# RG-LRU gate products: the two 64-feature blocks on the two halves of TensorE's rows

## Chip, cores and metric
The kernel runs on one core of one Trainium2 chip. The metric is device microseconds of one execution. In the profile PE is TensorE (PEld its weight loads), DVE is VectorE, ACT is ScalarE, POOL is GpSimd, and SP issues nearly all DMAs.

## Reference
A two-layer trunk over 256 latent and 256 context tokens with 2048 features. Each layer normalizes and modulates, projects into three branches, and projects back with a gated residual. The change touches the first branch, the RG-LRU, whose 512 features stand in 8 blocks of 64:

```python
ub = u.reshape(bsz, t_len, N_BLK_A, BLK_A)
gate_r = sigmoid(einsum('btni,nij->btnj', ub, w_r).reshape(bsz, t_len, D_A) + b_r)
gate_i = sigmoid(einsum('btni,nij->btnj', ub, w_i).reshape(bsz, t_len, D_A) + b_i)
log_a = -LRU_C * gate_r * softplus(-lam)
a = exp(log_a)
b = sqrt(-expm1(2.0 * log_a)) * (gate_i * u)
...
h = associative_scan(a * h + b)
```

Each gate multiplies every block of 64 features of u by a 64x64 matrix of its own. This is done for two directions of time and two layers. u is the branch's input after a convolution over four tokens.

## The kernel before
All tensors lie with features on the 128 partitions and the 512 tokens (256 latent, 256 context) on the free axis. A branch of 512 features is four tiles t, and a tile holds two of the 64-feature blocks.

*Projections.* `project` makes one tile of 128 output features from 16 input tiles. The weights come in chunks of 512 columns, four to a tile (`Weights.ahead`, three chunks ahead). ACT casts a chunk to a high half `wh`, DVE makes the low half `wl`, and each of four input tiles takes three matmuls (`accumulate`): wh by xh, wl by xh, wh by xl, all in the kernel's reduced fp32 type (F32R). In layer 1 the tiles that need no context stream 256 tokens in place of 512 (narrow tiles).

*Background work.* Between pairs of input tiles, `between` lets `Background.pump` run one step of each of three lanes: gated DeltaNet heads (lane 0), attention heads and RG-LRU tiles (lane 1), the short preparations (lane 2). The steps are Python generators, and each `yield` ends one. Which step runs where is decided by a cost model of the engines' clocks (class `Timed`). It also lets DVE fill its spare time with the products of the modulation weights (`macc`). The tile framework then orders the instructions of each engine by its own estimates. All instructions are recorded in one helper, so the profile puts them on line 89 and they are told apart by tile names.

*RG-LRU.* `consume` calls `rglru` (line 945) when one of the tiles xa0 to xa3 is projected. It runs the convolution on ACT and DVE, loads the gate weights `rgt`, and queues `rglru_scan` (line 951) in lane 1. That splits u into two halves `us` and, for each direction d, the weights into two halves `rg`. For each gate g, `product3` makes three matmuls of 128 rows, 128 columns and 512 tokens into a PSUM bank `pg` (pool `pb`, two banks), and ACT reads the bank with a tanh and the bias `hb`:

```python
for g, dst in ((0, a), (1, gu)):
    pg = pb_()
    product3(pg, [x[:, P * g:P * g + P] for x in rg], us)
    act.activation(out=dst, in_=pg, func=AF.Tanh, scale=0.5, bias=hb[:, 8 * g + j:8 * g + j + 1])
    yield
```

The weights of a gate are a 128x128 matrix with the two blocks on its diagonal and zeros elsewhere (`w_rg` in `kernel`). After the gates come a tanh (`m2sp`) and an exp (`m4sp`) on ACT, products on DVE, one Sqrt on ACT for both directions (with a table load before it), and the scans over time on DVE. There are 16 such groups of two gates: 2 layers, 4 tiles, 2 directions.

Of the kernel before, what the change touches and what calls it, by code (L numbers as in the profile page):

```python
# [10 lines left out]
AF = mybir.ActivationFunctionType  # L11
ALU = mybir.AluOpType

P = 128
KT = 16
T = 256
TT = 512
# [77 lines left out]
def trunk(ctx, tc, xT, cT, consts, masks, rope_t, small, fg, w_mod0, w_mod, w_first, w_in, w_ba, w_rg, w_out, out):  # L95
    nc = tc.nc
    pe, dve, act, pool = Timed(nc.tensor, "pe"), Timed(nc.vector, "dve"), Timed(nc.scalar, "act"), Timed(nc.gpsimd, "pool")
# [9 lines left out]
    def psum(tag, shape=(P, TT), bufs=2):  # L107
        return ps.tile(list(shape), F32, tag=tag, name=tag, bufs=bufs)
# [3 lines left out]
    def tmp(tag, shape=(P, TT), bufs=None, dt=F32):  # L112
        return wk.tile(list(shape), dt, tag=tag, name=tag, bufs=bufs or BUFS.get(tag, 2))
# [7 lines left out]
    def pb_():  # L121
        return psum("pb", bufs=2)
# [18 lines left out]
    for k in range(KT):  # L141
        y = big.tile([P, TT], F32, tag=f"Y{k}", name=f"Y{k}")
# [217 lines left out]
    def split(a, hi=None, lo=None):  # L360

        n = a.shape[1]
        hi = tmp("wb", dt=F32R)[:, 0:n] if hi is None else hi
        lo = tmp("wb", dt=F32R)[:, 0:n] if lo is None else lo
        act.copy(out=hi, in_=a)
        dve.tensor_tensor(out=lo, in0=a, in1=hi.bitcast(F32), op=ALU.subtract)
        return hi, lo

    def product3(out, a, b):

        for i, (x, y) in enumerate(((0, 0), (1, 0), (0, 1))):
            pe.matmul(out=out, lhsT=a[x], rhs=b[y], start=(i == 0), stop=(i == 2))
# [60 lines left out]
    def conv(pz, wc, halves, bias=None, tag="u"):  # L433
        n = len(halves)
        act.copy(out=zp[:, 0:n, 2:2 + T], in_=pz[:, 0:n * T].rearrange("p (s t) -> p s t", s=n))
        u = tmp(tag)
        uv = u[:, 0:n * T].rearrange("p (s t) -> p s t", s=n)
        if bias is None:
            act.activation(out=uv, in_=zp[:, 0:n, 0:T], func=AF.Copy, scale=wc[:, 0:1])
        else:  # L440
            act.activation(out=uv, in_=zp[:, 0:n, 0:T], func=AF.Identity, scale=wc[:, 0:1], bias=bias)
        for j in range(1, 4):
            dve.scalar_tensor_tensor(out=uv, in0=zp[:, 0:n, j:j + T], scalar=wc[:, j:j + 1], in1=uv, op0=ALU.mult, op1=ALU.add)
        return u
# [158 lines left out]
    def layer(l, acc, bs):  # L603
# [22 lines left out]
        hb = big.tile([P, 16], F32, tag="hb", name="hb")  # L626
# [11 lines left out]
        def yt(k):  # L638
            if ydst[k] is None:
                Y[k] = big.tile([P, TT], F32, tag=f"Y{k}", name=f"Y{k}")  # L640
                ydst[k] = Y[k]
            return ydst[k]
# [4 lines left out]
        def branch_result(k, src, cc, scale=None):  # L647

            ready.add(k)
            y = yt(k)[:, cc]  # L650
            if k in gated:
                dve.scalar_tensor_tensor(out=y, in0=src, scalar=0.5 if scale is None else scale, in1=y, op0=ALU.mult, op1=ALU.mult)
            elif scale is None:
                act.copy(out=y, in_=src)
            else:
                act.activation(out=y, in_=src, func=AF.Copy, scale=scale)
# [287 lines left out]

        def rglru(t, pz):
            u = conv(pz, s[:, S_CA + 4 * t:S_CA + 4 * t + 4], (0, 1), bias=s[:, S_CAB + t:S_CAB + t + 1], tag="wb")
            rgt = tmp("wa")
            nc.sync.dma_start(out=rgt, in_=w_rg[l, t].rearrange("p d g j -> p (d g j)"))
            bg.add(1, t, rglru_scan(t, u, rgt))

        def rglru_scan(t, u, rgt):
            us = split(u)
            th = tmp("th", (P, 2, TT), bufs=1)
            ab = []
            for d in range(2):
                j = 4 * d + t
                rg = tmp("wb", dt=F32R)
                rg = split(rgt[:, T * d:T * d + T], rg[:, 0:T], rg[:, T:TT])
                yield
                a, gu = tmp("wb"), tmp("wb")  # L960
                for g, dst in ((0, a), (1, gu)):
                    pg = pb_()
                    product3(pg, [x[:, P * g:P * g + P] for x in rg], us)
                    act.activation(out=dst, in_=pg, func=AF.Tanh, scale=0.5, bias=hb[:, 8 * g + j:8 * g + j + 1])
                    yield
                dve.scalar_tensor_tensor(out=gu, in0=gu, scalar=1.0, in1=u, op0=ALU.add, op1=ALU.mult)
                act.activation(out=th[:, d], in_=a, func=AF.Tanh, scale=m2sp[:, j:j + 1], bias=m2sp[:, j:j + 1])
                act.activation(out=a, in_=a, func=AF.Exp, scale=m4sp[:, j:j + 1], bias=m4sp[:, j:j + 1])
                dve.scalar_tensor_tensor(out=a, in0=a, scalar=1.0, in1=th[:, d], op0=ALU.add, op1=ALU.mult)
                dve.tensor_scalar(out=a, in0=a, scalar1=1.0, scalar2=None, op0=ALU.add)  # L970
                ab.append((a, gu))
                yield
            act.activation(out=th, in_=th, func=AF.Sqrt, scale=-1.0, bias=tiny)
            yield
            for d, (a, b) in enumerate(ab):
                dve.scalar_tensor_tensor(out=th[:, d], in0=a, scalar=1.0, in1=th[:, d], op0=ALU.add, op1=ALU.mult)
                dve.scalar_tensor_tensor(out=b, in0=b, scalar=0.5, in1=th[:, d], op0=ALU.mult, op1=ALU.mult)
                yield
                hh = th[:, d]
                if d == 0:  # L980
                    dve.tensor_tensor_scan(out=hh[:, T:TT], data0=a[:, T:TT], data1=b[:, T:TT], initial=0.0, op0=ALU.mult, op1=ALU.add)
                    dve.tensor_tensor_scan(out=hh[:, 0:T], data0=a[:, 0:T], data1=b[:, 0:T], initial=hh[:, TT - 1:TT], op0=ALU.mult, op1=ALU.add)
                else:
                    for a0, ini in ((T, 0.0), (0, hh[:, T:T + 1])):
                        r = lambda x: x[:, a0:a0 + T][:, ::-1]
                        dve.tensor_tensor_scan(out=r(hh), data0=r(a), data1=r(b), initial=ini, op0=ALU.mult, op1=ALU.add)
                yield
            if t in gated:
                dve.tensor_tensor(out=th[:, 0, 0:nq], in0=th[:, 0, 0:nq], in1=th[:, 1, 0:nq], op=ALU.add)
                branch_result(t, th[:, 0, 0:nq], slice(0, nq))  # L990
            else:
                dve.tensor_tensor(out=yt(t), in0=th[:, 0, 0:nq], in1=th[:, 1, 0:nq], op=ALU.add)
                ready.add(t)
# [166 lines left out]
        for n in range(KT):  # L1160
# [5 lines left out]
            if last:  # L1166
                y = Y[n][:, 0:T]
# [14 lines left out]
    for k in range(KT):  # L1182
        square_into(acc, Y[k], k, TT, dve)
    gw = []
    acc = layer(0, acc, None)
    mod_finish(((1, 0), (1, 1)))
    acc = layer(1, acc, gw[0])
# [86 lines left out]
```

## Time and profile before

| | us |
|---|---|
| median of 3 runs (1531.92 to 1535.7) | 1533.33 |
| the profiled execution | 1529.33 |
| its span on the core | 1527.5 |
| PE busy | 1466.9 |
| DVE busy | 1165.8 |
| ACT busy | 739.9 |
| mean granted TensorE clock | 0.994 |

The span goes from the first to the last instruction, and 1.8 us of the execution lie outside it. A timeline row gives the start of a group of equal instructions and how long they took from the first start to the last end. Matmuls overlap their neighbours, so the distance between two starts tells what one costs in a stream, not its duration. The RG-LRU tiles run from about 590 to 700 us (layer 0) and from 1340 to 1420 us (layer 1).

### The profile page before, as it was taken

The numbers are of one execution on the slowest core, as the hardware profiler recorded it, in microseconds if no ns is written. First come the engines' busy times: TensorE is split into PE (matmuls) and PEld (weight loads), VectorE is DVE, ScalarE is ACT, GpSimd is POOL, SyncE is SP. The second block draws the span as 40 slices with busy tenths as digits, with TensorE's granted clock in tenths as the row PEclk, the third lists the DMA queues.
The fourth block names the chain that finished last, engine by engine and source line by source line (L and its number), as shares of the span: only waits on it lengthen the run. The fifth ranks groups of instructions, "written<-read, shape, count | busy, mean of one in ns | idle before, by whom it ended". The sixth has DMA issues, their size and how long they took to land.

```text
span 1527.5 us, 29952 instructions
## 1 busy us (share of the span) xinstructions
PE 1466.9 (96%) x11762; PEld 1206.4 (79%) x11762; DVE 1165.8 (76%) x2513; ACT 739.9 (48%) x1708; POOL 113.2 (7%) x114
## 2 busy tenths in 40 slices
PE   4999999999999999999999999999999999999996
PEld 3777678787877877788888887877977889779996
DVE  4445989889898898999648876887885776788755
ACT  3323445454444546655422224554544555677653
POOL 0000100100010010000011110010200100000011
PEclk9999999999999999999999999999999999999998
DMA  9997544444443453345446655545552333234553
GB/s 345 332 347 256 152 127 144 128 135 130 144 149 113 145 177 116 107 143 160 136 127 224 212 188 196 187 146 170 183 178 64 104 115 104 81 98 131 190 189 113
DMA packets 90686, 247.68 MB, mean 162 GB/s; under 512 B 9200, under 2 KB 20912, under 8 KB 90544
## 3 DMA queue, kind: packets, MB, share of 16 engines
q1 hardware_dynamic: 89392, 244.71, 49.2%
q8 instruction: 92, 1.51, 0.4%
q10 hardware_dynamic: 1152, 1.05, 0.2%
q14 instruction: 50, 0.41, 0.1%
HBM read 243.60 MB, written 2.13 MB: 161 GB/s over the span
## 4 chain that ended last, share of the span: by engine, by line
PE 82%; DVE 10%; ACT 3%; DMA 2%; issue 1%; POOL 1%; SPq 0%; DVEq 0%; ACTq 0%; POOLq 0%
PE pz L89 58%; PE pa L89 9%; PE pb L89 8%; PE pt L89 4%; PE pm L89 3%; DVE wb L89 2%; DVE wl L89 1%; DVE macc L89 1%; DMA wraw<-in_w_in 1%; DVE th L89 1%; DVE o L89 1%; ACT t L89 1%; ACT wb L89 1%; DMA wa<-rows_d 1%; DVE u L89 1%
## 5 line engine op out<-in xcount | busy, mean ns | idle before, releaser
L89 PE MATMUL pz<-xh,wh 128*128 128x512 f32 (+1 forms) x1760 | 645.1, 367 | 2.5 <-ACT xh L89 2.4
L89 PE MATMUL pz<-xh,wl 128*128 128x512 f32 (+1 forms) x1760 | 629.4, 358 | 0.8 <-DVE wl L89 0.8
L89 PE MATMUL pz<-xl,wh 128*128 128x512 f32 (+1 forms) x1760 | 628.8, 357 | 0.0
L89 ACT CAST wh<-wraw 128x512 fp32r<-128x512 f32 x488 | 293.1, 612 | 335.5 <-PE pz L89 206.2
L89 DVE TENSOR_TENSOR wl<-wraw,wh 128x512 fp32r<-128x512 f32 x488 | 328.2, 681 | 133.0 <-ACT wh L89 131.7
L89 PEld LDWEIGHTS pz<-xh,wh 128*128 128x128 f32 x1760 | 331.8, 189 | 53.0 <-ACT xh L89 8.6
L89 PEld LDWEIGHTS pz<-xl,wh 128*128 128x128 f32 x1760 | 331.9, 189 | 50.4 <-DVE xl L89 3.5
L89 PEld LDWEIGHTS pz<-xh,wl 128*128 128x128 f32 x1760 | 332.6, 189 | 42.5 <-DVE wl L89 1.2
L89 DVE SCALAR_TENSOR_TENSOR macc<-wm,cs,macc 128x512 f32<-128x512 f32 x400 | 293.3, 766 | 2.1 <-DMA wm<-in_w_mod 1.6
L89 PE MATMUL pb<-wb 128*128 128x128 f32 (+1 forms) x560 | 112.5, 328 | 3.8 <-ACT wb L89 2.0
L89 PEld LDWEIGHTS pb<-wb 128*128 128x128 f32 x560 | 79.6, 190 | 16.9 <-ACT wb L89 7.0
L89 DVE TENSOR_SCALAR modA<-pm,nb,small 128x2 f32<-128x2 f32 x16 | 4.5, 279 | 69.2 <-PE pm L89 69.2
L89 POOL TENSOR_TENSOR o<-o,t 128x512 f32<-128x512 f32 (+1 forms) x28 | 30.4, 1086 | 325.7 <-ACT t L89 325.7
L89 ACT ACTIVATE wb<-pb,mx,rqa 128x512 f32<-128x512 f32 (+1 forms) x48 | 33.9, 707 | 42.4 <-DVE mx L89 42.1
L89 DVE SCALAR_TENSOR_TENSOR u<-zp,small,u 128x512 f32<-128x512 f32 (+1 forms) x72 | 50.6, 702 | 1.9 <-ACT u L89 1.6
L89 ACT ACTIVATE xh<-u,modS 128x256 fp32r<-128x256 f32 x64 | 30.9, 506 | 39.7 <-DVE u L89 39.6
L89 ACT ACTIVATE t<-pt 128x128 f32<-128x128 f32 (+1 forms) x122 | 34.2, 280 | 32.8 <-PE pt L89 30.7
L89 PEld LDWEIGHTS pa<-c,s 32*32 32x32 f32 x2304 | 24.9, 107 | 21.8 <-issue 13.0
L89 ACT COPY s<-pm 128x128 f32<-128x128 f32 x16 | 4.3, 266 | 67.0 <-PE pm L89 67.0
L89 DVE TENSOR_REDUCE mx<-pb 128x1 f32<-128x512 f32 (+1 forms) x48 | 28.8, 599 | 10.0 <-PE pb L89 9.6
L89 POOL TENSOR_TENSOR rqa<-rqa,mhalf 128x4 f32<-128x4 f32 (+1 forms) x16 | 17.3, 1084 | 243.6 <-DVE rqa L89 243.6
L89 ACT COPY wb<-pb 128x512 f32<-128x512 f32 (+1 forms) x48 | 24.7, 515 | 21.4 <-PE pb L89 20.9
(260 smaller groups left out, 1816.8 us busy)
## 6 DMA issues: line engine op xcount, KB each, us to landing
wraw<-in_w_in SPq DMA_DIRECT2D x148, 512.0 KB, 3.6
wm<-in_w_mod SPq DMA_DIRECT2D x128, 512.0 KB, 3.7
wraw<-in_w_out SPq DMA_DIRECT2D x64, 512.0 KB, 3.6
wraw<-in_w_first SPq DMA_DIRECT2D x32, 448.0 KB, 5.0
wb<-in_w_mod SPq DMA_DIRECT2D x48, 256.0 KB, 6.3
kq<-in_w_mod SPq DMA_DIRECT2D x16, 512.0 KB, 6.3
Y<-in_xT SPq DMA_DIRECT2D x16, 256.0 KB, 5.4
wa<-in_w_mod SPq DMA_DIRECT2D x16, 256.0 KB, 6.8
```

The source lines that it names most:

```text
L89: return f(*args, **kw)
```

## The change
A gate no longer fills a 128x128 matrix with two blocks and zeros. For each block b (the rows 64b to 64b + 63) the weights are now 64 rows by 128 columns, one gate's 64 columns beside the other's: gate r first for block 0, gate i first for block 1. Three matmuls on the upper half of TensorE's rows go into one PSUM bank, and three on the lower half (`tile_position` 64) into the other. The two halves take turns. A bank then holds both gates of one block, so ACT reads each gate in two halves of 64 partitions. For gate i each half is read from the other half's partitions, and the biases are rolled to match. The number of matmuls stays at 96, the tanh reads go from 32 to 64, and the gate weights halve, which also halves their loads (8 DMAs), their casts (16) and their low halves (16). The yields stay as many; the first step now holds all six matmuls.

```diff
@@ -944,9 +944,11 @@
 
         def rglru(t, pz):
             u = conv(pz, s[:, S_CA + 4 * t:S_CA + 4 * t + 4], (0, 1), bias=s[:, S_CAB + t:S_CAB + t + 1], tag="wb")
-            rgt = tmp("wa")
-            nc.sync.dma_start(out=rgt, in_=w_rg[l, t].rearrange("p d g j -> p (d g j)"))
+            rgt = tmp("wa")[:, 0:2 * P]
+            nc.sync.dma_start(out=rgt, in_=w_rg[l, t].rearrange("p d j -> p (d j)"))
             bg.add(1, t, rglru_scan(t, u, rgt))
+
+        halves = (slice(0, 64), slice(64, P))
 
         def rglru_scan(t, u, rgt):
             us = split(u)
@@ -955,14 +957,22 @@
             for d in range(2):
                 j = 4 * d + t
                 rg = tmp("wb", dt=F32R)
-                rg = split(rgt[:, T * d:T * d + T], rg[:, 0:T], rg[:, T:TT])
+                rg = split(rgt[:, P * d:P * d + P], rg[:, 0:P], rg[:, P:2 * P])
                 yield
                 a, gu = tmp("wb"), tmp("wb")
-                for g, dst in ((0, a), (1, gu)):
-                    pg = pb_()
-                    product3(pg, [x[:, P * g:P * g + P] for x in rg], us)
-                    act.activation(out=dst, in_=pg, func=AF.Tanh, scale=0.5, bias=hb[:, 8 * g + j:8 * g + j + 1])
-                    yield
+
+
+                pg = [pb_(), pb_()]
+                for i, (x, y) in enumerate(((0, 0), (1, 0), (0, 1))):
+                    for b, hf in enumerate(halves):
+                        pe.matmul(out=pg[b], lhsT=rg[x][hf], rhs=us[y][hf], start=(i == 0), stop=(i == 2), tile_position=(64 * b, 0))
+                for b, hf in enumerate(halves):
+                    act.activation(out=a[hf], in_=pg[b][hf], func=AF.Tanh, scale=0.5, bias=hb[hf, j:j + 1])
+                yield
+                for b, hf in enumerate(halves):
+                    other = halves[1 - b]
+                    act.activation(out=gu[hf], in_=pg[b][other], func=AF.Tanh, scale=0.5, bias=hb[other, 8 + j:9 + j])
+                yield
                 dve.scalar_tensor_tensor(out=gu, in0=gu, scalar=1.0, in1=u, op0=ALU.add, op1=ALU.mult)
                 act.activation(out=th[:, d], in_=a, func=AF.Tanh, scale=m2sp[:, j:j + 1], bias=m2sp[:, j:j + 1])
                 act.activation(out=a, in_=a, func=AF.Exp, scale=m4sp[:, j:j + 1], bias=m4sp[:, j:j + 1])
@@ -1245,17 +1255,18 @@
     w_first = np.concatenate([w_in[..., c:c + P] for c in cols[0][:NSTART]], -1)
     w_ba = w_in[..., BA0:BA0 + 16].transpose(0, 2, 1, 3).reshape(L, P, 256)
     w_out_t = a["w_out"].reshape(L, 2, 8, P, KT, P).transpose(0, 4, 1, 3, 2, 5).reshape(L, KT, 2, P, 1024)
-    w_rg = np.zeros((L, 4, P, 2, 2, P), np.float32)
+    w_rg = np.zeros((L, 4, P, 2, P), np.float32)
     for g, name in enumerate(("w_ra", "w_ia")):
         w = a[name].reshape(L, 2, 4, 2, 64, 64)
         for b in range(2):
-            w_rg[:, :, 64 * b:64 * b + 64, :, g, 64 * b:64 * b + 64] = w[:, :, :, b].transpose(0, 2, 3, 1, 4)
+            c = 64 * (g ^ b)
+            w_rg[:, :, 64 * b:64 * b + 64, :, c:c + 64] = w[:, :, :, b].transpose(0, 2, 3, 1, 4)
     rep = lambda v: np.broadcast_to(v.reshape(L, 1, 8), (L, P, 8))
     small = np.concatenate([
         feat(a["norm_g"]), feat(a["b_mod"]),
         a["conv_a_w"].reshape(L, 4, 4, P).transpose(0, 3, 2, 1).reshape(L, P, 16), feat(a["conv_a_b"]),
         a["conv_b_w"].reshape(L, 4, 12, P).transpose(0, 3, 2, 1).reshape(L, P, 48),
-        feat(a["b_ra"]).transpose(0, 2, 1, 3).reshape(L, P, 8), feat(a["b_ia"]).transpose(0, 2, 1, 3).reshape(L, P, 8),
+        feat(a["b_ra"]).transpose(0, 2, 1, 3).reshape(L, P, 8), np.roll(feat(a["b_ia"]).transpose(0, 2, 1, 3).reshape(L, P, 8), 64, 1),
         feat(a["lam_a"]).transpose(0, 2, 1, 3).reshape(L, P, 8),
         rep(a["a_log_b"]), rep(a["dt_bias_b"]),
         a["onorm_b"][:, :, None], a["qn_c"][:, :, None], a["kn_c"][:, :, None]], 2)
```

The other instructions of every engine keep their number, but they are reordered from shortly before the first group on. First PE, in layer 0: the first group (tile 0, direction 0) among the matmuls of a projection (`pz`). `pb` are the gate banks, `wb_6504` is u's high half (transposes and attention use `pb` too), `wb_6505` its low half, `wb_6509` the gate weights. `pm` and `pa` are the modulation's and the DeltaNet head's products. Before:

```order
L89 MATMUL pz_6623<-xl12_1393,wh_6624 128x512
L89 MATMUL pz_6623<-xh13_1494,wh_6624 128x512
L89 MATMUL pb_6547<-wb_6504,wb_6509 128x512
L89 MATMUL pb_6568<-wb_6504,wb_6509 128x512
L89 MATMUL pb_6547<-wb_6504,wb_6509 128x512
L89 MATMUL pb_6547<-wb_6505,wb_6509 128x512
L89 MATMUL pb_6568<-wb_6504,wb_6509 128x512
L89 MATMUL pb_6568<-wb_6505,wb_6509 128x512
L89 MATMUL pz_6623<-xh13_1494,wl_6625 128x512
L89 MATMUL pz_6623<-xl13_1495,wh_6624 128x512
L89 MATMUL pm_4669<-macc_6097,sel_117 2x128 x8
```

With the change:

```order
L89 MATMUL pz_6633<-xh14_1569,wh_6634 128x512
L89 MATMUL pz_6633<-xh14_1569,wl_6635 128x512
L89 MATMUL pb_6547<-wb_6504,wb_6509 128x512
L89 MATMUL pb_6548<-wb_6504,wb_6509 128x512
L89 MATMUL pz_6633<-xl14_1570,wh_6634 128x512
L89 MATMUL pb_6547<-wb_6504,wb_6509 128x512
L89 MATMUL pb_6548<-wb_6504,wb_6509 128x512
L89 MATMUL pb_6547<-wb_6505,wb_6509 128x512
L89 MATMUL pb_6548<-wb_6505,wb_6509 128x512
L89 MATMUL pz_6633<-xh15_1644,wh_6634 128x512
L89 MATMUL pz_6633<-xh15_1644,wl_6635 128x512
```

The two gates of three became three pairs, one matmul for each bank, and the first pair stands apart from the others by one `pz` matmul. Of the 16 groups ten are in one piece, four are cut 2 and 4 like this one, one 2, 2 and 2, and one 3 and 3.

Second ACT, in layer 1: tile 2, the second direction's gates and what follows, with the casts of the weight chunks (`wh`). Before:

```order
L89 CAST wh_15114<-wraw_15112 128x512
L89 COPY full_14508<-pa_15092 64x4x64
L89 ACTIVATE wb_15127<-pb_15129,hb_9623 128x512
L89 ACTIVATE th_14875<-wb_15127,m2sp_9620 128x512
L89 CAST wh_15151<-wraw_15112 128x512
L89 ACTIVATE s_15141<-pa_15125,bb_14366 128x128
L89 ACTIVATE s_15144<-pa_15126,bb_14366 128x128
L89 ACTIVATE wb_15127<-wb_15127,m4sp_9619 128x512
L89 ACTIVATE wb_15128<-pb_15146,hb_9623 128x512
L89 ACT_TABLE_LOAD
L89 ACTIVATE th_14875<-th_14875,tiny_124 128x1024
L89 CAST wh_15188<-wraw_15186 128x512
```

With the change, from the cast after this group's reads:

```order
L89 CAST wh_15188<-wraw_15186 128x512
L89 COPY full_14582<-pa_15167 64x4x64
L89 ACTIVATE th_14842<-wb_15128,m2sp_9636 128x512
L89 ACTIVATE wb_15128<-wb_15128,m4sp_9635 128x512
L89 COPY zp_111<-pz_15085 128x2x256
L89 ACTIVATE s_15213<-pa_15199,bb_14382 128x128
L89 ACTIVATE s_15216<-pa_15200,bb_14382 128x128
L89 ACT_TABLE_LOAD
L89 ACTIVATE th_14842<-th_14842,tiny_124 128x1024
L89 ACTIVATE wb_15229<-zp_111,small1_74 128x512
L89 CAST wh_15237<-wraw_15186 128x512
```

The four reads of 64x512 stand ahead of the first cast shown; before, the second read stood behind the cast in the middle. Six instructions stood between the last two casts; now nine do. A copy of the next RG-LRU tile (`zp`) and its first convolution tap (`small1`) moved in between.

## Rows read from the trace of the kernel before
**Rows 1.** The page, busy time (share, instructions); chain that ended last, by engine.
```profile
PE 1466.9 (96%) x11762; PEld 1206.4 (79%) x11762; DVE 1165.8 (76%) x2513; ACT 739.9 (48%) x1708; POOL 113.2 (7%) x114
...
PE 82%; DVE 10%; ACT 3%; DMA 2%; issue 1%; POOL 1%; SPq 0%; DVEq 0%; ACTq 0%; POOLq 0%
```

**Rows 2.** Windows: busy us by engine, granted clock, DMA share, GB/s.
```profile
590.00:700.00 110.00, 109.40 (x868) 85.44 (x867) 103.11 (x201) 69.10 (x128) 2.26 (x2) 1.00 0.38 119
1340.00:1420.00 80.00, 76.85 (x702) 70.30 (x703) 67.84 (x142) 59.73 (x112) 0.71 (x1) 1.00 0.39 124
```

**Rows 3.** Timeline of DVE: start us, us, operation; low halves of two weight chunks.
```profile
620.50 0.69 DVE L89 TENSOR_TENSOR wl<-wraw,wh 128x512 fp32r<-128x512 f32 x1
...
1344.65 0.69 DVE L89 TENSOR_TENSOR wl<-wraw,wh 128x512 fp32r<-128x512 f32 x1
```

**Rows 4.** Timeline of PE: start us, us, operation; where those chunks are first used.
```profile
621.98 0.40 PE L89 MATMUL pz<-xh,wl 128*128 128x512 f32 x1
...
1345.39 0.38 PE L89 MATMUL pz<-xh,wl 128*128 128x256 f32 x1
```

**Rows 5.** Timeline of PE, 1340 to 1420 us: its waits [idle before <-releaser].
```profile
1350.47 0.73 PE L89 MATMUL pb<-wb 128*128 128x512 f32 x2 [1.39 <-ACT wb L89]
1352.33 1.19 PE L89 MATMUL pb<-wb 128*128 128x512 f32 x4 [1.12 <-DVE wb L89]
...
1379.49 0.39 PE L89 MATMUL pz<-xh,wl 128*128 128x256 f32 x1 [0.54 <-DVE wl L89]
```

**Rows 6.** Timeline of PE, layer 0: four gate matmuls and the next.
```profile
599.93 1.09 PE L89 MATMUL pb<-wb 128*128 128x512 f32 x4
600.86 0.39 PE L89 MATMUL pz<-xh,wh 128*128 128x512 f32 x1
```

**Rows 7.** Timeline of PE, layer 1: eight full 128-column matmuls and the next.
```profile
1203.26 1.10 PE L89 MATMUL pb<-wb 128*128 128x128 f32 x8
1204.11 0.47 PE L89 MATMUL pz<-xh,wh 128*128 128x512 f32 x1
```

**Rows 8.** Timeline of PE, layer 0: a run of 64x64 matmuls and its neighbours.
```profile
633.79 0.40 PE L89 MATMUL pz<-xl,wh 128*128 128x512 f32 x1
634.11 0.68 PE L89 MATMUL pa<-c,wa 64*64 64x64 f32 x16
634.72 0.50 PE L89 MATMUL pz<-xh,wh 128*128 128x512 f32 x1
635.06 0.39 PE L89 MATMUL pz<-xh,wl 128*128 128x512 f32 x1
```

**Rows 9.** Groups by form: operation, form, count | busy us, mean ns | idle.
```profile
L89 ACT ACTIVATE s<-pa,bb 128x128 f32<-128x128 f32 x96 | 28.7, 369 | 10.6 <-PE pa L89 10.5
...
L89 ACT ACT_TABLE_LOAD x17 | 21.8, 1283 | 3.8 <-DVE th L89 2.8 <-PEq L1266 0.7
...
L89 ACT ACTIVATE wb<-pb,hb 128x512 f32<-128x512 f32 x32 | 21.4, 685 | 12.2 <-PE pb L89 12.0
...
L89 ACT COPY zp<-pz 128x512 f32<-128x512 f32 x27 | 15.9, 587 | 31.1 <-PE pz L89 30.9
...
L89 ACT ACTIVATE wb<-wb,m4sp 128x512 f32<-128x512 f32 x16 | 13.0, 814 | 0.1
...
L89 ACT ACTIVATE th<-th,tiny 128x1024 f32<-128x1024 f32 x8 | 9.2, 1153 | 0.1
...
L89 DVE TENSOR_TENSOR wb<-wa,wb 128x256 fp32r<-128x256 f32 x16 | 6.7, 419 | 0.2
...
L89 ACT COPY full<-c 32x256 f32<-32x256 f32 x16 | 6.5, 404 | 4.8 <-DVE c L89 4.6
L89 ACT CAST wb<-wa 128x256 fp32r<-128x256 f32 x16 | 6.5, 403 | 0.0
...
L89 ACT COPY o<-pa 128x128 f32<-128x128 f32 x24 | 6.2, 266 | 7.4 <-PE pa L89 7.0
```

**Rows 10.** DMA issues: out<-in, queue, count, KB each, us to landing.
```profile
wa<-in_w_rg SPq DMA_DIRECT2D x8, 256.0 KB, 2.6
```

## Prediction
> **What bounds the kernel now.** I read the page first. PE is busy for 1466.9 us, 96% of the span, and the chain of waits runs through PE for 82% and through DVE for 10% [rows 1]. So the first question is how much PE time the change takes away. The second is whether PE stays the last one to arrive in the two stretches that hold the gate products. For that I read the windows table: in layer 0 (590 to 700 us) PE is busy for 109.4 of 110 us, DVE for 103.1 and ACT for 69.1. In layer 1 (1340 to 1420 us) it is 76.9, 67.8 and 59.7 of 80. The granted clock is 1.00 in both, the 2.4 GHz level [rows 2]. The reader should see that DVE has 7 us to spare in layer 0 and ACT some 20 us in layer 1. Shares hide how late a supply is, so I next read the timeline for the moment at which a weight chunk is ready and the moment at which PE takes it. Its low half (wl) is written at 620.50 + 0.69 = 621.19 us, and at 1344.65 + 0.69 = 1345.34 us [rows 3]; PE starts on these at 621.98 and 1345.39 [rows 4]. (Which chunk is which I counted back from the layer's last tile, four chunks a tile, in queue order.) The lead is 0.8 and 0.05 us. At 1379.49 PE waits 0.54 us for such a chunk, and at 1350 and 1352 it waits 1.39 and 1.12 us for the gates' own operands [rows 5]. So PE is the bound, with a supply just behind it at a few places.
>
> **What a gate product costs on PE.** There are 16 groups (2 layers, 4 tiles, 2 directions) of 6 matmuls, 96 before and 96 now. Four of them take from 599.93 to 600.86 us, 0.2325 each [rows 6], so a group takes 1.395 us and all 22.3 us. Now each covers half of the rows, and the two halves come in turn. If two halves stream side by side, 3 steps do the work of 6.
>
> *Do they?* No row of before has two row halves over the same columns. The nearest are the 64x64 products, where the halves also have different columns. Eight full matmuls of 128 columns take from 1203.26 to 1204.11, 0.106 each [rows 7]; 64 columns at that rate are 0.053, so 16 in a row would be 0.85 us. From the matmul before them (633.79) to the second one after (635.06) are 1.27 us [rows 8]. Less two plain matmuls (0.465) that leaves 0.805 for all 16 and their overhead, so they do overlap. I take full overlap: 96 become 48 steps, and one group that the order cuts into 3 and 3 needs 4 steps. 47 x 0.2325 = 10.9 us are saved. The other end is 0, no overlap.
> The Trainium skill, "TensorE: Matmul & The Clock Gate", section "Measured speedup vs the span model", gives 3.07 times for four row tiles of 512 columns, not 4. At that efficiency two tiles would give 1.54 times, and the sum below would come out 3.1 us higher (an estimate from that page); no row here shows it, and I go by the 64x64 rows.
>
> *What changing over costs.* The step into the 64x64 run is 634.11 - 633.79 = 0.32 against 0.23, and the first matmul after it takes 635.06 - 634.72 = 0.34 until the next: 0.09 + 0.105 = 0.195 us that are plainly seen. At most it is 0.805 less 8 steps of 0.053 = 0.38 [rows 8]. The gate matmuls of before pay none of this, as they are full like their neighbours. I take 0.30 for each run. The order of PE after the change has 23 such runs (counted there): ten groups in one piece, four cut 2 and 4, one 2, 2 and 2, one 3 and 3. 23 x 0.30 = 6.9 us (4.5 to 8.7).
>
> *PE together:* -10.9 + 6.9 = **-4.0 us**, from -6.4 to -2.2.
>
> **ACT and DVE.** The 32 tanh reads of 128x512 take 21.4 us, 0.669 each [rows 9]. They become 64 of 64x512. Fewer partitions don't make an instruction shorter: a copy of 32x256 takes 404 ns, a cast of 128x256 403 [rows 9]. So 32 more cost 21.4 us. The 16 casts of 128x256 fall from 0.403 to about 0.26 (a 128x128 copy takes 266 ns), -2.3 us; ACT gets +19 us, 9.5 in each layer. In layer 1 its load goes from 59.7 to 69 of 80 us. DVE's 16 low halves (0.419 each) shrink likewise, about -2 us, on an engine that PE rarely waits for; I count nothing. The cover of the ACT work is the lead of the weight chunks, and ACT is strictly in order: behind the four reads stand the casts of the next chunks (wh), which DVE's wl and then PE wait for. Where the lead is over 1.3 us, four reads in place of two (+1.34) cost nothing; where it is thinner, they cost up to 1.34 a group. Two groups of layer 0 stand just ahead of the 0.8 us lead at 622: +2.7. In layer 1 the order of ACT changes after the third tile's second group. Between two wh casts stood 6 instructions (two s reads of 0.369, m4sp 0.814, a tanh read, the table load 1.283, sqrt 1.153: 4.7 us); now stand 9, with m2sp, m4sp, a zp copy of 0.587, a convolution's first tap of about 0.81 and a 0.40 copy: 6.6 us [rows 9]. That is +1.9 just ahead of the place where PE already waits (1379). The two groups at 1350 wait for their own operands, behind which the lead recovers: 0. **Given back: +4.6 us**, between 0 and 10.7 (all eight groups of layer 1).
>
> **Queues, DMA, order.** The eight gate loads on SP halve, 256 to 128 KB each. They land in 2.6 us, far ahead of use [rows 10]: 0. No other instruction is added: the rest has the same counts on every engine. Both pb banks are now held until four reads are done, 4 x 0.669 = 2.7 us; the next group stands at least a conv cast and 15 matmuls (3.5 us) later in the order where I looked: 0, up to 1 if it comes sooner. The neighbours are reordered. That may remove or double the three PE waits of 3.05 us [rows 5], so +-3, and I take 0.
>
> **Sum.** -4.0 + 4.6 = +0.6 us on the profiled execution of 1529.3 (span 1527.5), whose place is 4.0 under the median of 1533.33. On the median: **1533.9 us**, its own range 1528 to 1540. About 0.3%, 4.6 us, is what a measurement of this kernel can tell from no change.
>
> **Rivals.**
> *Cheap change-over (faster).* Row halves use all columns, as the full array does, and have the same number type; the runs of before differ from their neighbours in columns and in type. If nothing is lost at the borders, PE saves the full 10.9 us, and after the same 4.6 given back it is -6.3: 1527.0. For it: nothing in the rows separates the causes of the 0.195. Against it: the 0.09 of entry is there at 64x64 whatever follows.
> *The supply starves (slower).* The place is ACT in layer 1, from the second tile on, where PE takes narrow chunks, of 256 tokens [rows 4]. It decides as soon as the four reads and the sqrt with its table load leave no cast in between for longer than the lead. The price is all eight groups there, 8 x 1.34 = 10.7, with the layer-0 2.7: -4.0 + 13.4 = +9.4, so 1542.7. For it: leads of 0.05 to 0.8 us [rows 3, 4]. Against it: ACT keeps 11 of 80 us free even then.
> The Trainium skill, "TensorEngine Tiling (Array Packing)", section "PSUM Bottleneck", warns of this: tiling speeds up TensorE, not the reads out of PSUM. The ACT rows agree as far as the price of a read goes; that it decides here is not shown.
> *The halves run one after the other (slower).* Then the change does not do what it is named for: PE saves nothing, pays 6.9, and as PE is later, only half of the 4.6 counts: +9.2, 1542.5. For it: no row with shared columns. Against it: the 64x64 halves overlap.
>
> **How the numbers follow.** Forecast 0.52, cheap change-over 0.19, starved supply 0.17, one after the other 0.12. Of the forecast's 0.52, 0.06 falls under -4.6 us, 0.05 over +4.6. Faster: 0.19 + 0.06 = 0.25. Slower: 0.05 + 0.16 + 0.12 = 0.33, as 0.01 of the starved supply stays within. Same: 0.42. The range reaches from just under the fast rival to the two slow ones, 1526 to 1543; half of each slow case and a little of the fast one lie outside.
>
> **What would show it.** Right: gate groups in one piece take about 0.7 us for six, 0.3 us more with their borders; pairs start within a few ns of each other; 64 reads of about 0.67 us; the same PE waits as before, and one or two more for wl near 620 and 1379. Wrong: six starts 0.23 apart (no overlap), no longer step at the borders (cheap change-over), or ACT above 90% in 1340 to 1420 with several PE waits for wl (starved). A time under 1528.7 or over 1538 would make the forecast wrong.

## The result and the profile after

| | before | with the change |
|---|---|---|
| median, us | 1533.88 (4 runs, 1531.92 to 1535.70) | 1543.52 (4 runs, 1542.15 to 1545.99) |
| ratio | | 1.0064, 95% interval 1.0047 to 1.0080 |
| the profiled execution, its span | 1529.33, 1527.5 | 1542.63, 1540.8 |

The change makes the kernel slower by 0.64%. The page of the profile after, busy time by engine, and the chain that ended last by engine:

```profile
PE 1468.8 (95%) x11762; PEld 1199.5 (78%) x11762; DVE 1163.4 (76%) x2513; ACT 760.5 (49%) x1740; POOL 112.4 (7%) x114
...
PE 75%; DVE 11%; ACT 6%; DMA 5%; issue 2%; POOL 1%; SPq 0%; DVEq 0%; ACTq 0%; POOLq 0%
```

PE's share of the chain falls from 82% [rows 1] to 75%, while ACT's doubles to 6%. PE loses time without having more to do: between these two executions, which lie further apart than the medians, the span grows by 13.3 us and PE's busy time by 1.9. The rest is idle time. The windows of the two stretches with gate products, two around 1360 us and four after 1375 (busy us by engine PE, PEld, DVE, ACT, POOL; granted clock, DMA share, GB/s):

```profile
590.00:700.00 110.00, 107.77 (x848) 79.64 (x847) 103.88 (x202) 77.58 (x141) 2.33 (x2) 1.00 0.39 123
1340.00:1420.00 80.00, 71.88 (x735) 61.31 (x735) 58.26 (x126) 62.98 (x112) 0.71 (x1) 0.94 0.31 96
1355.00:1360.00 5.00, 3.27 (x16) 2.14 (x14) 5.00 (x12) 3.12 (x6) 0.00 (x0) 1.00 0.22 82
1360.00:1365.00 5.00, 4.93 (x46) 3.46 (x47) 4.67 (x11) 4.77 (x9) 0.00 (x0) 0.66 0.50 141
1375.00:1380.00 5.00, 5.00 (x38) 4.64 (x37) 1.74 (x5) 4.91 (x8) 0.00 (x0) 1.00 0.00 2
1380.00:1385.00 5.00, 2.22 (x19) 2.02 (x18) 5.00 (x9) 2.67 (x5) 0.00 (x0) 1.00 0.00 0
1385.00:1390.00 5.00, 2.80 (x12) 2.67 (x13) 5.00 (x10) 0.82 (x2) 0.00 (x0) 0.52 0.34 102
1390.00:1395.00 5.00, 5.00 (x34) 4.47 (x34) 3.28 (x10) 4.39 (x8) 0.00 (x0) 0.80 0.36 111
```

In 1340 to 1420 us PE is idle for 8.1 us, where it was 3.15 [rows 2], and neither DVE (58 of 80) nor ACT (63) is full. So no engine's load fills this stretch. (This window, the prediction's, leaves out the start of layer 1's RG-LRU: u of the first tile is cast at 1310.22 us before and at 1313.29 now.) From 1375 on, DVE and ACT take turns at being full: ACT 4.9 of 5 us while DVE does 1.7, then DVE 5 of 5 while ACT falls to 0.8. That alternation looks like a chain between the two.

To see where the time is lost, I counted the projection matmuls of both traces and took the difference of the start of the same one. Ahead of the first changed instruction it is 0.7 us. It is 2.9 behind the RG-LRU of layer 0, again 2.8 at 1376 us (in between the new order lets it swing from -3.4 to 3.2), 11.9 at 1418 us, and 12.8 at the end. So layer 1 pays, within some 40 us. The timeline of PE there:

```profile
1381.82 0.40 PE L89 MATMUL pz<-xh,wh 128*128 128x256 f32 x2
1387.20 0.58 PE L89 MATMUL pz<-xh,wl 128*128 128x256 f32 x1 [4.98 <-DVE wl L89]
1387.58 0.41 PE L89 MATMUL pz<-xl,wh 128*128 128x256 f32 x1
1387.79 0.42 PE L89 MATMUL pz<-xh,wh 128*128 128x256 f32 x1
```

PE waits 4.98 us for one low half of a weight chunk; such a long wait is called a hole below. It is the place of the 0.54 us wait of before (1379.49 [rows 5]). After the wait the steps of 256 tokens are 0.21 us long: the granted clock stands at 0.52 in 1385 to 1390 (about the 1.2 GHz level) and at 0.80 in the next 5 us, so the lower clock cost PE some 0.48 x 2.80 + 0.20 x 5.00 = 2.3 us more. At 1360 to 1365, behind two waits of 0.68 and 1.05 us, it stands at 0.66, which is another 0.34 x 4.93 = 1.7 us. Before, it was 1.00 in all of 1340 to 1420 [rows 2], so of the 9 to 10 us that layer 1 loses some 4.0 (an estimate from these rows) are lost to the clock in and after waits. What DVE did meanwhile (timeline of DVE):

```profile
1379.93 1.29 DVE L89 SCALAR_TENSOR_TENSOR th<-wb,th 128x512 f32<-128x512 f32 x2 [1.63 <-ACT th L89]
1381.14 1.29 DVE L89 SCALAR_TENSOR_TENSOR wb<-wb,th 128x512 f32<-128x512 f32 x2
1382.35 1.27 DVE L89 TENSOR_TENSOR_SCAN th<-wb 128x256 f32<-128x256 f32 x2
1383.53 1.37 DVE L89 TENSOR_TENSOR_SCAN th<-wb,th 128x256 f32<-128x256 f32 x2
1384.82 0.73 DVE L89 SCALAR_TENSOR_TENSOR wb<-zp,small,wb 128x512 f32<-128x512 f32 x1
1385.46 0.42 DVE L89 TENSOR_TENSOR Y<-th 128x256 f32<-128x256 f32 x1
1385.79 0.75 DVE L89 SCALAR_TENSOR_TENSOR wb<-zp,small,wb 128x512 f32<-128x512 f32 x1
1386.46 0.68 DVE L89 TENSOR_TENSOR wl<-wraw,wh 128x512 fp32r<-128x512 f32 x1
```

Eleven instructions of RG-LRU work, 6.5 us, stand ahead of the `wl` that PE wants: the products and scans of tile xa2 and two convolution taps of xa3. They are issued together, because tile xa3 is just projected and `consume` asks for all that is left of xa2. They begin only when ACT's Sqrt of xa2 (`th`) is there. ACT's Sqrts of xa0 to xa2 (timelines of ACT, before and with the change; those of xa3 stand further below, at 1401.81 and 1416.09):

```profile
1325.26 1.15 ACT L89 ACTIVATE th<-th,tiny 128x1024 f32<-128x1024 f32 x1
...
1344.69 1.16 ACT L89 ACTIVATE th<-th,tiny 128x1024 f32<-128x1024 f32 x1
...
1369.10 1.15 ACT L89 ACTIVATE th<-th,tiny 128x1024 f32<-128x1024 f32 x1
```
```profile
1330.73 1.15 ACT L89 ACTIVATE th<-th,tiny 128x1024 f32<-128x1024 f32 x1
...
1352.42 1.15 ACT L89 ACTIVATE th<-th,tiny 128x1024 f32<-128x1024 f32 x1
...
1378.75 1.15 ACT L89 ACTIVATE th<-th,tiny 128x1024 f32<-128x1024 f32 x1
```

Each is later by more than the one ahead of it: 5.5, 7.7, 9.7 and 14.3 us. The whole layer starts 3.1 us later (1313.29 against 1310.22). Less that, the first three Sqrts are late by 2.4, 4.7 and 6.6 us at a time when PE's projections are not: 2.9 at 1300, 2.8 at 1376. So the tiles fall behind PE first, and PE waits for them after.

**The matmuls themselves.** The timeline of PE in layer 0, one group in one piece and one pair by itself:

```profile
659.54 0.40 PE L89 MATMUL pz<-xl,wh 128*128 128x512 f32 x1
659.86 0.96 PE L89 MATMUL pb<-wb 64*128 64x512 f32 x6
660.76 0.50 PE L89 MATMUL pz<-xh,wh 128*128 128x512 f32 x1
661.09 0.39 PE L89 MATMUL pz<-xh,wl 128*128 128x512 f32 x1
```
```profile
619.23 0.40 PE L89 MATMUL pz<-xh,wl 128*128 128x512 f32 x1
619.57 0.50 PE L89 MATMUL pb<-wb 64*128 64x512 f32 x2
620.00 0.50 PE L89 MATMUL pz<-xl,wh 128*128 128x512 f32 x1
620.33 0.39 PE L89 MATMUL pz<-xh,wh 128*128 128x512 f32 x1
```

From the full matmul ahead to the second one behind, the six take 661.09 - 659.54 = 1.55 us, less two plain ones (0.465) 1.085; full matmuls took 1.395. The pair takes 620.33 - 619.23 - 0.465 = 0.635, where two full ones take 0.465. The difference of the two, 0.45, is two steps of 0.225. So the halves do run side by side, at one plain step for a pair (their starts lie 1 to 13 ns apart in the trace), and a run costs 0.635 - 0.2325 = 0.40 us for changing over. A cut-off pair is a loss of 0.17. A run of four that one full matmul parts from a pair did worse still (the row ahead of it and the second one behind, timeline of PE):

```profile
599.86 0.51 PE L89 MATMUL pz<-xl,wh 128*128 128x512 f32 x1
...
601.30 0.40 PE L89 MATMUL pz<-xh,wl 128*128 128x512 f32 x1
```

That is 601.30 - 599.86 - 0.465 = 0.975 for four, where full matmuls take 0.93: 0.51 for changing over.

**The reads.** Groups by form after, ACT (count | busy us, mean ns | idle before):

```profile
L89 ACT ACTIVATE wb<-pb,hb 64x512 f32<-64x512 f32 x64 | 43.7, 683 | 9.8 <-PE pb L89 8.6
...
L89 ACT CAST wb<-wa 128x128 fp32r<-128x128 f32 x16 | 4.7, 293 | 0.0
```

Half the partitions, the same time: 683 ns against 685 [rows 9]. The casts have half the columns and take 293 ns where they took 403 [rows 9].

### The profile page after: what moved, and what is told of

Same layout as the page of the kernel before. It is cut to its first block, busy times and chain, and to the rows that moved or that the text cites. A ratio compares the mean times of both kernels' runs of the same rounds, so it can differ in the third digit from the quotient of the medians.

```text
span 1540.8 us, 29997 instructions
## 1 busy us (share of the span) xinstructions
PE 1468.8 (95%) x11762; PEld 1199.5 (78%) x11762; DVE 1163.4 (76%) x2513; ACT 760.5 (49%) x1740; POOL 112.4 (7%) x114
## 3 DMA queue, kind: packets, MB, share of 16 engines
q8 instruction: 92, 1.51, 0.4%
q10 hardware_dynamic: 1152, 1.05, 0.2%
## 4 chain that ended last, share of the span: by engine, by line
PE 75%; DVE 11%; ACT 6%; DMA 5%; issue 2%; POOL 1%; SPq 0%; DVEq 0%; ACTq 0%; POOLq 0%
PE pz L89 53%; PE pa L89 9%; PE pb L89 7%; PE pt L89 4%; PE pm L89 3%; ACT wb L89 2%; DVE wl L89 2%; DVE wb L89 2%; DMA wraw<-in_w_in 1%; DVE macc L89 1%; DVE th L89 1%; ACT wh L89 1%; ACT t L89 1%; DMA wb<-in_w_mod 1%; DVE u L89 1%
## 5 line engine op out<-in xcount | busy, mean ns | idle before, releaser
L89 PE MATMUL pb<-wb 128*128 128x128 f32 (+2 forms) x560 | 101.9, 336 | 4.8 <-DVE wb L89 3.0
L89 PEld LDWEIGHTS pb<-wb 128*128 128x128 f32 (+1 forms) x560 | 70.9, 190 | 20.2 <-ACT wb L89 7.6
L89 ACT ACTIVATE wb<-pb,hb 64x512 f32<-64x512 f32 x64 | 43.7, 683 | 9.8 <-PE pb L89 8.6
```

Source lines behind the costliest of these rows:

```text
L89: return f(*args, **kw)
```

## Experiments

Two theories at first. **R**: the 32 extra reads hold up the RG-LRU chain. **O**: putting six matmuls into one step, and the order that follows, does. A third, **C**, blames the changing over on PE. From experiment 5 on R is split in two. **L** (latency): the reads lengthen the way to a tile's Sqrt. **A**: ACT's load counts, wherever the reads stand. Ratios are to the kernel before on the same chip, with their 95% intervals.

| | kernel | median us | ratio |
|---|---|---|---|
| 1 | full matmuls, one step, whole reads | 1538.17 | 1.0034 (1.0022 to 1.0046) |
| 2 | full matmuls, one step, half reads | 1543.47 | 1.0065 (1.0047 to 1.0083) |
| 3 | the change, whole reads | 1534.15 | 1.0011 (0.9999 to 1.0023) |
| 4 | before, half reads | 1548.83 | 1.0104 (1.0088 to 1.0120) |
| 5 | the change, gate i read later | 1548.75 | 1.0101 (1.0082 to 1.0120) |
| 6 | the change, gb3 ahead of xa2 | 1543.01 | 1.0062 (1.0048 to 1.0076) |
| 7 | before, gb3 ahead of xa2 | 1538.65 | 1.0039 (1.0024 to 1.0054) |
| 8 | the change, narrow tiles spread | 1544.70 | 1.0074 (1.0059 to 1.0089) |
| 9 | the change, ga2 ahead of xa3 | 1543.12 | 1.0061 (1.0047 to 1.0075) |
| 10 | before, ga2 ahead of xa3 | 1534.98 | 1.0011 (1.0002 to 1.0021) |
| 11 | the change, 14 casts on GpSimd | 1544.20 | 1.0075 (1.0058 to 1.0092) |
| 12 | before, 14 casts on GpSimd | 1536.10 | 1.0023 (1.0012 to 1.0034) |
| 13 | the change, half reads in layer 1 alone | 1544.43 | 1.0075 (1.0057 to 1.0093) |
| 14 | the change, half reads in layer 0 alone | 1533.84 | 1.0002 (0.9989 to 1.0015) |
| 15 | as 3, a product on GpSimd in the chain | 1539.29 | 1.0045 (1.0028 to 1.0061) |
| 16 | the change, ACT dearer in the planner | 1553.20 | 1.0130 (1.0109 to 1.0150) |
| 17 | before, ACT dearer in the planner | 1548.14 | 1.0087 (1.0071 to 1.0103) |

### Experiments 1 to 4: the step, the matmuls, the reads
Experiment 1, against the kernel before:

```diff
-for g, dst in ((0, a), (1, gu)):
-    pg = pb_()
-    product3(pg, [x[:, P * g:P * g + P] for x in rg], us)
-    act.activation(out=dst, in_=pg, func=AF.Tanh, scale=0.5, bias=hb[:, 8 * g + j:8 * g + j + 1])
-    yield
+pg = [pb_(), pb_()]
+for g in range(2):
+    product3(pg[g], [x[:, P * g:P * g + P] for x in rg], us)
+act.activation(out=a, in_=pg[0], func=AF.Tanh, scale=0.5, bias=hb[:, j:j + 1])
+yield
+act.activation(out=gu, in_=pg[1], func=AF.Tanh, scale=0.5, bias=hb[:, 8 + j:9 + j])
+yield
```

Experiment 2 is experiment 1 with each of its reads in two halves (`for hf in halves`, and `a[hf]`, `pg[0][hf]`, `hb[hf, ...]`). Experiment 4 does the same to the kernel before. Experiment 3, against the change:

```diff
-for b, hf in enumerate(halves):
-    act.activation(out=a[hf], in_=pg[b][hf], func=AF.Tanh, scale=0.5, bias=hb[hf, j:j + 1])
+act.activation(out=a, in_=pg[0], func=AF.Tanh, scale=0.5, bias=hb[:, j:j + 1])
 yield
-for b, hf in enumerate(halves):
-    other = halves[1 - b]
-    act.activation(out=gu[hf], in_=pg[b][other], func=AF.Tanh, scale=0.5, bias=hb[other, 8 + j:9 + j])
+act.activation(out=gu, in_=pg[1], func=AF.Tanh, scale=0.5, bias=hb[:, 8 + j:9 + j])
 yield
```

> Full matmuls and whole 128-row reads as before, but both gates' six matmuls are issued in one step of the background lane, as in the change. Theory R (the 32 extra reads hold up the RG-LRU chain on ACT, so that DVE's block of RG-LRU work lands ahead of a weight chunk that PE needs): 1532 to 1536 us, no PE wait for wl over 1 us near 1380. Theory O (putting all six matmuls in one step, and the order that follows from it, is what makes the block): 1541 to 1546, a PE wait for wl of 3 us or more near 1380. Theory C (changing over between full and half-row matmuls costs the time): 1532 to 1536.

> Full matmuls, six in one step, and four reads of 64 rows in place of two of 128. Theory R: 1541 to 1547, with the PE wait for wl of 3 us or more in layer 1. Theory O: 1541 to 1547 too, but no more than experiment 1. Theory C: 1532 to 1537.

> The half-row matmuls of the change, but each bank is read once and whole (128 rows), so one gate's values of the second block are swapped with the other's: the gate activations are not the reference's, all other work is. Theory R: 1530 to 1534 (the PE saving of about 1.9 us shows, no wait for wl over 1 us near 1380). Theory O: 1541 to 1545. Theory C: 1540 to 1545, without a wait for wl.

> The kernel before with its steps and full matmuls; only each read of 128 rows becomes two of 64. Theory R: 1541 to 1547, with a PE wait for wl of 3 us or more in layer 1. Theory O: 1533 to 1536. Theory C: 1533 to 1536.

Taken one after the other these kernels give: one step +0.34% (5.2 us), half-row matmuls on top of that -0.23% (from 1.0034 to 1.0011, 3.5 us), half reads on top of both +0.53% (8.1 us). That they add up to the change's +0.64% is by construction, as each is the distance from one kernel to the next. In another order the parts have other sizes. Half reads cost +0.31% (4.8 us) from experiment 1 to 2 and +1.04% (16 us) from before to experiment 4. With half reads in place, one step gains 0.39% (from 4 to 2), and half-row matmuls gain nothing (from 2, at 1.0065, to the change). What all three pairs agree on is that half reads cost time. In these four the long wait for `wl` near 1385 us goes with the reads (timelines of PE, one row each from experiments 2 and 4):

```profile
1384.04 0.58 PE L89 MATMUL pz<-xh,wl 128*128 128x256 f32 x1 [3.45 <-DVE wl L89]
```
```profile
1389.08 0.39 PE L89 MATMUL pz<-xh,wl 128*128 128x256 f32 x1 [3.33 <-DVE wl L89]
```

In experiments 1 and 3 PE is busy for 19.66 and 20.00 of the 20 us from 1375 to 1395. So R stands, though its ranges missed experiments 1 (1538 for 1532 to 1536) and 4 (1549 for 1541 to 1547). O explains no hole. What one step costs depends on the rest: 5.2 us in experiment 1, while experiment 3, which has it too, comes to 1.0011. C falls: experiment 3 was to take 1540 to 1545.

### Experiments 5 to 12: load, latency or place?
Three cures were tried. Experiment 5 moves the second yield and gate i's reads behind `m4sp` and its two DVE instructions. Experiments 6, 8 and 9 give PE narrow tiles earlier (7 and 10 are the controls on the kernel before). The end of layer 1's tile order, as it was and then in experiments 6, 8 and 9:

```diff
-xa0 xa1 xa2 gb3 gb0 xa3 ga2 gc7 ga3 ga1 gc5 ga0 gc4
+xa0 xa1 gb3 xa2 gb0 xa3 ga2 gc7 ga3 ga1 gc5 ga0 gc4
+xa0 gb3 xa1 gb0 xa2 ga2 xa3 gc7 ga3 ga1 gc5 ga0 gc4
+xa0 xa1 xa2 gb3 gb0 ga2 xa3 gc7 ga3 ga1 gc5 ga0 gc4
```

Experiment 11 (12 on the kernel before) takes casts away from ACT, 14 of the 28 around layer 1's RG-LRU tiles (the line of the cast alone is shown; `on_pool` picks the 14):

```diff
-act.copy(out=wh[:, 0:n], in_=raw)
+(pool.tensor_copy if on_pool else act.copy)(out=wh[:, 0:n], in_=raw)
```

> The change, but gate i's two reads are issued one step later, behind m2sp and m4sp, so that they no longer stand between gate r's reads and the Sqrt of a tile; the number of reads stays 64. Theory L (latency: the reads lengthen the way to the Sqrt, and DVE's block of RG-LRU work behind the Sqrt comes too late): 1532 to 1538 us, no PE wait for wl over 1.5 us between 1375 and 1395. Theory A (ACT's total load in these stretches counts, wherever the reads stand): 1541 to 1547, with the wait for wl of 3 us or more.

> The change, with the order of layer 1's tiles altered in one place: the narrow gate tile gb3 is projected ahead of xa2 in place of behind it, so that PE has some 5.7 us more work before tile xa2 asks for the rest of the RG-LRU tile ahead of it. Theory L: the hole is gone or under 1.5 us, 1533 to 1539. Theory A: the block of DVE work meets narrow weight chunks at another place, 1541 to 1547.

> The kernel before with the same altered tile order, as the control for experiment 6. Both theories: within 1530 to 1537, as the kernel before has no hole to lose.

> The change with one narrow gate tile between every two of the xa tiles of layer 1 (gb3, gb0 and ga2 move ahead). Theory L: PE has more work ahead of each tile's Sqrt, no wait for wl over 1.5 us in layer 1, 1531 to 1538. Theory A: 1541 to 1547.

> The change with the narrow gate tile ga2 projected ahead of xa3 in place of behind it: the hole stands where xa3 is done and the rest of xa2's RG-LRU is issued in one piece, so this gives xa2's chain 5.7 us more PE work to hide behind. Theory L (the chain of one tile is too long for the PE work up to the next one): the wait for wl at that place falls under 1.5 us, 1533 to 1539. Theory A (the waits come back elsewhere, as ACT's load stays): 1541 to 1547.

> The kernel before with the same altered tile order, the control for experiment 9. Theory L: 1530 to 1536, the small wait for wl (0.54 us) goes. Theory A: 1531 to 1537.

> The change with 14 of the 28 weight casts around the RG-LRU tiles of layer 1 (tiles xa1, xa2, gb3, gb0, xa3, ga2, gc7) moved from ACT to GpSimd: ACT has 14 x 0.61 = 8.5 us less to do in that stretch, and the gate reads stay 64. Theory A: 1534 to 1539, the wait for wl under 2 us. Theory L: the reads still stand in the chain, 1540 to 1546, wait for wl 3 us or more.

> The kernel before with the same 14 casts on GpSimd, the control for experiment 11. Theory A and theory L: 1531 to 1537, as ACT is not what PE waits for there; over that, GpSimd's casts come too late for the low halves.

None of them helped, and L's forecasts (1531 to 1539) missed in 5, 6, 8 and 9. Experiment 6 was aimed badly: the hole belongs to the issue of xa2's rest when xa3 is projected, and moving gb3 away from between the two takes PE work out of just that place. Its control, experiment 7, loses 5 us too, and has a hole of the same kind with whole reads (timeline of PE):

```profile
1385.13 0.38 PE L89 MATMUL pz<-xh,wl 128*128 128x256 f32 x1 [3.43 <-DVE wl L89]
```

So half reads are one way to open this hole, and taking cover away from it another. Experiment 9 is aimed right: the wait near 1385 is gone, and the time is the same. The idle time comes back, among other places in 1425 to 1440 (windows of experiment 9):

```profile
1425.00:1440.00 15.00, 12.75 (x88) 11.93 (x88) 14.91 (x36) 9.70 (x25) 0.00 (x0) 0.89 0.40 130
```

Theory A, ACT's load, came near the time for 5, 6, 8 and 9 (1541 to 1547; experiment 5 took 1549). It fails at experiment 11, where 14 casts (0.61 us each on ACT) were taken off it and the hole stayed (timeline of PE, and GpSimd's casts among its groups by form):

```profile
1390.12 0.58 PE L90 MATMUL pz<-xh,wl 128*128 128x256 f32 x1 [4.40 <-DVE wl L90]
```
```profile
L90 POOL CAST wh<-wraw 128x512 fp32r<-128x512 f32 x14 | 12.0, 856 | 72.3 <-PE pz L90 61.0 <-issue 5.0 <-DVE wb L90 3.6
```

The control, experiment 12, loses 0.23% (3.5 us) to the move, so in experiment 11 the relief may have won that much back, but not the 8 us of the reads. In experiment 11 ACT is busy for 57.4 of 80 us in 1340 to 1420, less than before the change (59.7 [rows 2]), and the hole is there all the same. The test is not quite clean: beside GpSimd's casts two DVE instructions of the block ahead of that `wl` took 1.10 and 1.03 us in place of some 0.7, so about 0.7 of the 4.40 may be GpSimd's.

### Experiments 13 to 15: which layer, and the chain
Experiments 13 and 14 are experiment 3 in one layer and the change in the other (`split_reads = l == 1`, or 0). Each layer has its gate groups cut as in the change or as in experiment 3. Experiment 15 adds one line to experiment 3, ahead of `m2sp`:

```diff
+pool.tensor_tensor(out=a, in0=a, in1=a, op=ALU.mult)
```

> The change, but in layer 0 each bank is read once and whole (gate values of layer 0 are not the reference's there); layer 1 has the four reads. If layer 1 pays for the reads: 1540 to 1544, with the wait for wl of 3 us or more near 1385. If layer 0 pays: 1533 to 1537.

> The change, but in layer 1 each bank is read once and whole (gate values of layer 1 are not the reference's there); layer 0 has the four reads. If layer 1 pays for the reads: 1533 to 1537, without a wait for wl of 2 us or more. If layer 0 pays: 1540 to 1544.

> Experiment 3 (half-row matmuls, whole reads, 1534) with one product of 128x512 on GpSimd between gate r's read and m2sp in each direction (it squares the gate, so the values are not the reference's): by the rows of GpSimd some 1.1 to 1.4 us more in the chain, as the extra reads add 1.34, and nothing on ACT. Theory L (the chain's length counts): 1540 to 1547, with waits of 3 us or more in layer 1. Theory A (ACT's load counts): 1533 to 1537.

Layer 1 pays for the reads: 1.0075 with its half reads, 1.0002 without. The 16 extra reads of layer 0 cost nothing that can be measured. The rows of ACT show the length of layer 1's RG-LRU: from the cast of u in the first tile (xa0) to the Sqrt in the last one (xa3). Before, the change, experiment 3, experiment 14:

```profile
1310.22 0.62 ACT L89 CAST wb<-wb 128x512 fp32r<-128x512 f32 x1 [1.05 <-DVE wb L89]
...
1401.81 1.15 ACT L89 ACTIVATE th<-th,tiny 128x1024 f32<-128x1024 f32 x1
```
```profile
1313.29 0.62 ACT L89 CAST wb<-wb 128x512 fp32r<-128x512 f32 x1 [1.23 <-DVE wb L89]
...
1416.09 1.16 ACT L89 ACTIVATE th<-th,tiny 128x1024 f32<-128x1024 f32 x1
```
```profile
1314.55 0.62 ACT L89 CAST wb<-wb 128x512 fp32r<-128x512 f32 x1 [1.28 <-DVE wb L89]
...
1405.76 1.16 ACT L89 ACTIVATE th<-th,tiny 128x1024 f32<-128x1024 f32 x1
```
```profile
1316.20 0.62 ACT L89 CAST wb<-wb 128x512 fp32r<-128x512 f32 x1 [0.95 <-DVE wb L89]
...
1407.74 1.16 ACT L89 ACTIVATE th<-th,tiny 128x1024 f32<-128x1024 f32 x1
```

That is 91.6 us before, 102.8 with the change, 91.2 and 91.5 in experiments 3 and 14. The difference of 11.2 is close to eight groups times two reads of 0.67 (10.7). In the same way this stretch takes 103.3 us in experiment 13, 102.6 in 4, 102.3 in 11, 99.6 in 2 and 106.4 in 5: all between 1543 and 1549 us. With whole reads it takes 92.8 in experiment 1 (1538 us) and 93.8 in 12 (1536). Experiment 5 did not shorten the chain but lengthened it, which is why it fails as a test of latency.

This length goes with the time, but it is not shown to be its cause. PE's projections and its hole lie in it: of the 11.2 us, 6.6 were there at the Sqrt of xa2, and the rest came with PE's own delay. From experiment 1 to 2 the same reads add 6.8, not 10.7.

Experiment 15's stretch takes 95.2 us (+4.0 on experiment 3), and its time rises by 0.34% (5.2 us). That is above A's range (1533 to 1537) and below L's (1540 to 1547), and the waits of 3 us that L called for are not there: the longest in layer 1 is 1.51. GpSimd's product (1.04 us in this stretch) lies partly beside ACT's read of gate i, so that ACT waits some 0.4 to 0.6 us for it. Nor is it latency alone. Beside six of the eight products of layer 1 a DVE instruction takes 1.05 to 1.53 us in place of 0.68, 3.1 us in all (one such pair, timelines of POOL and DVE; then a group by form of DVE from 1310 to 1420 us, experiments 3 and 15):

```profile
1359.58 1.04 POOL L89 TENSOR_TENSOR wb<-wb 128x512 f32<-128x512 f32 x1 [13.87 <-ACT wb L89]
```
```profile
1359.64 1.53 DVE L89 TENSOR_TENSOR wl<-wraw,wh 128x512 fp32r<-128x512 f32 x1
```
```profile
L89 DVE SCALAR_TENSOR_TENSOR wb<-wb 128x512 f32<-128x512 f32 x8 | 5.4, 679 | 6.9 <-ACT wb L89 6.9
```
```profile
L89 DVE SCALAR_TENSOR_TENSOR wb<-wb 128x512 f32<-128x512 f32 x8 | 6.9, 859 | 5.2 <-ACT wb L89 5.2
```

So that the reads cost time, and in layer 1, is shown; that they do so by their latency is likely (experiment 11 speaks against the load), but not shown.

### Experiments 16 and 17: the planner's price
The cost model (`Timed`) counts a read of 512 as 0.53 us, and the trace has 0.68. Is the loss made by steps that are placed by too low a price?

```diff
-cost = 0.1 + n / 1200
+cost = 0.15 + n / 960
```

> The change, with the planner's price of an ACT instruction raised from 0.1 + n/1200 to 0.15 + n/960 us, so that a read of 512 counts 0.683 as in the trace. If the loss comes from steps placed by too low a price: 1533 to 1539, no wait for wl over 2 us. If the length of the chain decides whatever the plan: 1540 to 1548.

> The kernel before with the same price, the control for experiment 16: 1530 to 1540 by either theory, as its plan changes everywhere; only the distance to experiment 16 counts (under 4 us if the price decided, 7 us or more if the chain does).

The distance is 0.43% (6.6 us by the ratios, 5.1 by the medians): between the two forecasts, so this settles nothing. A price nearer to the trace makes both plans worse, and both kernels land above every range given for them.

## Why the prediction was wrong

- **Overlap: right.** Three steps do the work of six; a pair takes 0.225 us within a run.
- **Changing over: too low.** 0.40 a run and more, where I took 0.30 and had 0.38 as the top. 23 runs at 0.40 cost 9.2 us of the 10.9 saved, so PE saves 1.7 us at most by these rows, not 4.0. By the measured times experiment 3 against 1 gives -3.5 with a new order in it, the change against experiment 2 nothing. The efficiency of 3.07 in 4 that the Trainium skill, "TensorE: Matmul & The Clock Gate", section "Measured speedup vs the span model", gives for four tiles does not show in the plain step of a pair; here the loss sits at the start and the end of a run.
- **Reads on ACT: right** in count and size, 64 x 0.683 = 43.7 us against 42.8 forecast.
- **What the reads give back: the step that failed.** I took the lead of the next weight chunks as their cover, and put 2.7 us on layer 0, 1.9 on one place in layer 1, and 0 on the two groups at 1350, "behind which the lead recovers". Layer 0 gave back nothing that can be measured. Layer 1 gave back all: 8.1 us from experiment 3 to the change, 9.5 from 14 to the change, and a wait of 4.98 at the place of the 1.9. The lead of single chunks was the wrong thing to read. In layer 1 the four RG-LRU tiles form one chain through ACT, DVE and PE, since each must be done when the next is projected. Its lag behind PE grew by about 2 us with every tile, until nothing was left to hide it. 10.7 us, the sum over all eight groups, stood in the text as an end of the range. The waits at 1350 [rows 5], for the gates' own operands, may have been a hint: in layer 0 the longest such wait was of 0.32 us. But they did not grow with the change (0.68 and 1.05 us); the hole opened elsewhere.
- **The order: taken as 0 within 3 us.** This failed too. Issuing both gates in one step costs 5.2 us in experiment 1, where I had 0; on that way to the change the reads' miss is smaller (8.1 for 4.6). On the way through experiment 4 the reads cost 16 us and the step gains 6. I had costed the two banks' hold and the cuts, not the step. Why its price changes so is open. Experiment 1's trace, of its slowest execution, shows only a place: by the count of projection matmuls it loses 5.0 us in layer 1, with waits of 1.40 us for a `wl` (1353.08) and of 1.96 and 0.95 us for the gates' operands (1358 to 1360).
- **The rival "the supply starves"** gave 1542.7 for 1543.5 measured, and named the place (layer 1), the cause (four reads) and the price (8 x 1.34). That the figures meet so closely is partly luck: its 2.7 us of layer 0 did not come, PE's gain was smaller, and the new step stood in no sum. Its path was wrong: not ACT's casts between the reads run late, but DVE's low halves behind the block that waits for the Sqrt. Its sign, ACT above 90% and several PE waits for wl, did not come: ACT has 63 of 80 us, and there is one long wait. "The halves run one after the other" (1542.5) is excluded by the pair's rows, "cheap change-over" by the 0.40.

Open stay three things. Whether the reads cost by their latency or by ACT's load. Why no other tile order wins the time back, although seven narrow tiles of some 5.7 us stand behind xa3: experiments 6, 8 and 9 show that the waits move, not what would hold them off. And how much of the loss is the chain's length itself, how much the static order that puts a late block ahead of a weight chunk. No run beat the kernel before; experiment 14 (1.0002) equals it but needs gate reads in layer 1 that the layout does not allow.

## What to carry to other kernels

Before trading PE time for reads out of PSUM, find the chain that each read lies in and count how often it comes round in series; here engine shares (ACT had 20 us free) and the lead of one buffer did not show it. How much of an addition to such a chain counts has to be tried: the same 32 extra reads cost 4.8, 8.1 and 16 us in three settings. For the same reason parts that were measured one at a time need not add up. Row tiles paid in long runs only: six matmuls took 1.085 us for 1.395, the run of four 0.975 for 0.93, a pair 0.635 for 0.465.

## What the runs showed of the hardware

- Two row halves over the same 128 columns, into two banks, run at one plain step for a pair (0.225 to 0.23 us), but a run of them costs 0.40 us, in and out together, and 0.51 in the run of four shown. The 64x64 rows of before showed 0.195 plainly and allowed 0.38.
- A tanh of 64x512 out of PSUM takes 683 ns, one of 128x512 685: half the partitions saved nothing.
- After 5 us of idling PE's granted clock fell to 0.52 and 0.80 in the two windows that followed, and after waits of 0.68 and 1.05 us to 0.66 in the next. Before, after waits of 1.39 and 1.12 us at 1350 and 1352 [rows 5], it stayed at 1.00.
- Beside a GpSimd product or cast of 128x512 a DVE instruction of some 0.7 us could take 1.03 to 1.53 (experiments 11 and 15); without them, with the change and in experiment 3, no DVE instruction from 1310 to 1420 us took over 0.76.
